# A hybrid decoder layer on one core: experts taken four at a time instead of one by one

## Chip, cores and metric

One core of a Trainium2 chip. The metric is the device time of one execution in microseconds; the median of the runs counts.

## What is computed

One decoder layer over 256 tokens of width 1024, all in float32: a token mixer (sparse attention beside a recurrent branch), and then a mixture of 32 experts with two chosen per token. The change lies in the second part and in the step between the two:

```python
h = h + gt1 * (merged @ w_out[l])
xn2 = _rmsnorm(h, moe_norm_g[l]) * (1.0 + sc2) + sh2
moe = _hier_moe(xn2.reshape(B * S, D), ...)
h = h + gt2 * moe.reshape(B, S, D)

def _hier_moe(xt, wg_router, we_router, e_bias, w_gate, w_up, w_down):
    ...
    def body(acc, ew):
        wg, wu, wd, cw = ew
        hdn = jax.nn.silu(xt @ wg) * (xt @ wu)
        return acc + cw[:, None] * (hdn @ wd).astype(f32), None
    acc, _ = lax.scan(body, jnp.zeros((T, D), f32), (w_gate, w_up, w_down, combine.T))
```

Gate and up weights are 1024 x 512 for each expert, down weights 512 x 1024: 6 MiB an expert, 192 MiB in all.

## The kernel before, in words

*Memory and loads.* One big tile, the arena, holds nearly everything, and a planner in the kernel's own text gives out columns of it while the program is built (`Arena.alloc`). Weights come in a fixed list of loads of 1 MiB (2048 float32 columns in 128 partitions), issued on the SP queue by `pump` (L271 to L287, the DMA at L283) as soon as a place is free; `done` gives a load's place back and pumps again. An instruction on SP that waits for its place holds up all that stand behind it. Two more tiles, both called `more`, join the arena when the mixer's buffers end. The list's last part is the experts: gate in two halves, up in two halves, and then, one expert late, down in two halves; for the last expert the down halves are columns instead of rows (2 KB pieces instead of 8 KB).

*Between mixer and experts.* The output projection runs in 16 steps of twelve products of 128x256 (L520 to L522), its weights split beforehand into a high and a low part by ACT, DVE and POOL, four pairs ahead. The logits of the router (L1465) and the sum of squares (L1467) run beside it. A step `reorder` stands after the fifth of these steps: 16 small products (L1485) and a few DVE operations bring shift and scale of the second norm into another order of channels. Then come the turns of the residual to token rows (L1473), and the routing, a long chain of small DVE operations (L1556 to L1606).

*The experts.* Each expert has room for 32 tokens (`CAP`); an overflow loop after them is empty here. For every four experts `group` makes a one-hot matrix and gathers their tokens by products (`gather`, L1620, 16 products, shown as 32 records, since a float32 product is two records in the profile) into eight slices of 128 columns, 32 for each expert. Then, expert by expert: `gate_up` runs 16 products of 128x512 in TensorE's four column groups (L1645), two for gate and two for up, each half of the contraction; ACT copies them, `hidden` turns them by products (L1652) and applies the SwiGLU on DVE and ACT; `scatter_weights` makes the matrix that brings rows back to tokens (L1634 on POOL, L1636); `down` runs 8 products (L1667), multiplies with the gate of the residual (L1672), and `finish` adds the expert's rows to the tokens in PSUM (four products of 128x512, L1699). The last expert's down products go by columns (`down_cols`, L1678, L1679), and `finish` adds the residual (L1701) and stores.

*What sets the order.* The program is recorded in the order of the text and a scheduling layer moves instructions within limits; SP's order is the list's. The first expert needs routing, the gather and the first four loads; a place comes free when the last product that reads it is over.

## Time and profile before

| | |
|---|---|
| runs | 805.62, 805.63, 882.06 us; median 805.63 |
| profiled execution | 806.51 us |
| its span, first to last instruction | 804.7 us |
| mean granted clock of TensorE | 0.959 of 2.4 GHz |
| busy | PE 694.5, DVE 382.7, ACT 201.4, POOL 216.4 us |
| HBM | 261.45 MB moved, 325 GB/s over the span |

The profile is of one execution. Sums are made against its 806.51 us and its span. The rows below show times in us from the span's start; a granted clock of 1.00 is 2.4 GHz and 0.50 is 1.2 GHz; a DMA share of 1 is all 16 DMA engines at work. Busy time of PE comes from records whose ends are modelled, so four products side by side in column groups show as overlapping records.

### The profile page before, as it was taken

How to read it: one execution, taken by the hardware profiler on the slowest of the kernel's cores; microseconds unless marked ns; L12 is line 12 of the kernel's file. 1: busy time of each engine (PE TensorE's matmuls, PEld its weight loads, DVE VectorE, ACT ScalarE, POOL GpSimd, SP SyncE). 2: the span in 40 equal slices, each digit the busy share in tenths (PEclk: the TensorE clock that was granted, in tenths of full speed). 3: DMA queues.
4: the chain of work that ended last, by engine and by line, in shares of the span. 5: the costliest groups of instructions: out<-in, count | busy, mean ns of one | idle time of the engine just before them, and what ended most of it. 6: DMA issues, size and time to landing. Idle time of an engine off the chain costs nothing.

```text
span 804.7 us, 12679 instructions
## 1 busy us (share of the span) xinstructions
PE 694.5 (86%) x5013; PEld 418.0 (52%) x5013; DVE 382.7 (48%) x866; ACT 201.4 (25%) x438; POOL 216.4 (27%) x251
## 2 busy tenths in 40 slices
PE   5898767899899999989998969888788779788777
PEld 1786547567789898954444324343243234243222
DVE  2577899999848666334223542221221221221214
ACT  2465523334536433231111101111011001011000
POOL 1348847612744226401111001101101101101100
PEclk9899968999999999989999989999999999999999
DMA  9995414456788566649999999999999999999994
GB/s 334 386 302 182 157 53 131 144 211 213 260 283 286 198 235 248 231 165 407 421 421 420 422 421 421 419 421 421 421 421 420 423 420 421 421 420 422 420 418 155
DMA packets 62636, 261.45 MB, mean 325 GB/s; under 512 B 7760, under 2 KB 23120, under 8 KB 36208
## 3 DMA queue, kind: packets, MB, share of 16 engines
q1 hardware_dynamic: 62576, 260.63, 82.4%
q8 instruction: 40, 0.66, 0.3%
q14 instruction: 20, 0.16, 0.1%
HBM read 259.57 MB, written 1.05 MB: 324 GB/s over the span
## 4 chain that ended last, share of the span: by engine, by line
PE 44%; DMA 32%; DVE 16%; POOL 4%; issue 2%; ACT 1%; DVEq 0%; SPq 0%; POOLq 0%
DMA arena<-in_expert_w_gate_dram 10%; DMA arena<-in_expert_w_up_dram 10%; PE ps_e L1645 7%; PE acc L1699 6%; DMA arena<-in_expert_w_down_dram 5%; PE ps_a L554 3%; PE ps_e L1620 3%; PE ps_e L1667 3%; PE ps_g L520 3%; DMA more<-in_expert_w_up_dram 3%; DMA more<-in_expert_w_gate_dram 2%; PE ps_g L522 2%; PE ps_g L521 2%; DVE split L510 2%; PE ps_e L1652 2%
## 5 line engine op out<-in xcount | busy, mean ns | idle before, releaser
L1634 POOL TENSOR_SCALAR arena<-arena 128x128 f32<-128x128 f32 x64 | 52.2, 822 | 373.8 <-PE ps_e L1636 213.6
L1645 PE MATMUL ps_e<-arena 128*32 128x512 f32 x832 | 134.5, 601 | 16.7 <-DMA arena<-in_expert_w_up_dram 16.7
L1699 PE MATMUL acc<-arena 128*128 128x512 f32 x256 | 119.9, 611 | 31.6 <-DVE arena L1672 31.6
L1699 PEld LDWEIGHTS acc<-arena 128*128 128x128 f32 x256 | 46.7, 193 | 98.2 <-DVE arena L1672 50.0
L1655 DVE TENSOR_SCALAR arena<-arena 128x128 f32<-128x128 f32 x32 | 7.2, 226 | 171.9 <-ACT arena L1654 171.6
L1646 ACT COPY arena<-ps_e 128x512 f32<-128x512 f32 x32 | 18.8, 586 | 279.2 <-PE ps_e L1645 279.2
L1645 PEld LDWEIGHTS ps_e<-arena 128*32 128x32 f32 x832 | 31.9, 110 | 93.8 <-issue 59.2
L510 DVE TENSOR_TENSOR split<-arena,split 128x512 fp32r<-128x512 f32 x84 | 67.2, 807 | 23.3 <-ACT split L509 12.6
L507 POOL TENSOR_SCALAR split<-arena 128x512 fp32r<-128x512 f32 x50 | 39.6, 796 | 103.1 <-PE ps_g L521 29.6
L1667 PE MATMUL ps_e<-arena 128*32 128x512 f32 x400 | 62.2, 601 | 0.5 <-DMA arena<-in_expert_w_down_dram 0.5
L1672 DVE TENSOR_TENSOR arena<-ps_e,arena 128x512 f32<-128x512 f32 x62 | 40.3, 683 | 45.6 <-PE ps_e L1667 45.5
L1645 PE MATMUL ps_e<-more,arena 128*32 128x512 f32 x192 | 57.5, 606 | 2.7 <-DMA more<-in_expert_w_up_dram 2.7
L554 PE MATMUL ps_a<-split 128*128 128x256 f32 x360 | 51.6, 303 | 2.9 <-ACT split L466 1.9
L554 PEld LDWEIGHTS ps_a<-split 128*128 128x128 f32 x360 | 47.6, 204 | 10.3 <-issue 4.8
L1652 PEld LDWEIGHTS ps_e<-arena 128*128 128x128 f32 x256 | 31.1, 191 | 27.0 <-ACT arena L1646 25.7
L509 ACT CAST split<-arena 128x512 fp32r<-128x512 f32 x60 | 36.5, 616 | 33.4 <-PE ps_g L521 17.0
L522 PE MATMUL ps_a<-split 128*128 128x256 f32 (+1 forms) x112 | 37.4, 334 | 8.1 <-DVE split L510 4.2
L1620 PEld LDWEIGHTS ps_e<-arena,more 128*128 128x128 f32 x256 | 33.4, 206 | 16.7 <-ACT arena L1637 6.9
L1620 PE MATMUL ps_e<-arena,more 128*128 128x128 f32 x256 | 35.7, 294 | 7.0 <-DVE arena L1692 5.6
L510 POOL TENSOR_TENSOR split<-arena,split 128x512 fp32r<-128x512 f32 x26 | 36.1, 1392 | 15.1 <-ACT split L509 11.2
L520 PE MATMUL ps_g<-split 128*128 128x256 f32 x128 | 39.0, 305 | 0.0
L521 PE MATMUL ps_a<-split 128*128 128x256 f32 (+1 forms) x112 | 36.4, 325 | 2.6 <-POOL split L510 1.0
(358 smaller groups left out, 1265.6 us busy)
## 6 DMA issues: line engine op xcount, KB each, us to landing
arena<-in_expert_w_up_dram SPq DMA_DIRECT2D x52, 1024.0 KB, 19.8
arena<-in_expert_w_gate_dram SPq DMA_DIRECT2D x52, 1024.0 KB, 19.8
arena<-in_expert_w_down_dram SPq DMA_DIRECT2D x52, 1024.0 KB, 19.8
arena<-in_w_in_dram SPq DMA_DIRECT2D x18, 1024.0 KB, 8.8
arena<-in_ada_w_dram SPq DMA_DIRECT2D x16, 1024.0 KB, 6.0
more<-in_expert_w_up_dram SPq DMA_DIRECT2D x12, 1024.0 KB, 19.8
more<-in_expert_w_down_dram SPq DMA_DIRECT2D x12, 1024.0 KB, 19.8
more<-in_expert_w_gate_dram SPq DMA_DIRECT2D x12, 1024.0 KB, 19.9
```

The source lines that it names most:

```text
L510: (nc.gpsimd if p[1] == "P" else nc.vector).tensor_sub(l, w, h.bitcast(F32))
L520: nc.tensor.matmul(ps, l[0], r[0], start=start, stop=False)
L521: nc.tensor.matmul(ps, l[0], r[1], start=False, stop=False)
L522: nc.tensor.matmul(ps, l[1], r[0], start=False, stop=stop)
L554: nc.tensor.matmul(p, a[:, kk, :], b[:, 4 * hf + kk, :], start=(i == 0 and kk == KORD[0]), stop=(i == 2 and kk == KORD[-1]))
L1620: nc.tensor.matmul(ps[:, n * kk:n * kk + n], h2[:, a, 2 * k2 + kk, :], oh(a), start=(a == 0), stop=(a == 1))
L1634: nc.gpsimd.tensor_scalar(o4[:, a], io1[:, None, :].to_broadcast([128, 4, CAP]), rk_(a), cb(a), op0=OP.is_equal, op1=OP.mult)
L1645: nc.tensor.matmul(ps[32 * g:32 * g + 32, :], xg[:, kk, :], w[:, k, :], start=(k == 0), stop=(k == 3))
L1652: nc.tensor.matmul(ps[:, 64 * f:64 * f + 64], gu[:, 128 * f:128 * f + 128], SEL, start=True, stop=True)
L1667: nc.tensor.matmul(ps[c][32 * g:32 * g + 32, :], hT[:, 2 * i + j, :], wd[:, j, 512 * c:512 * c + 512], start=True, stop=True)
L1672: nc.vector.tensor_mul(Y4b[:, s], ps[c], gt2[0][:, s])
L1699: nc.tensor.matmul(o, stb[e % 2][:, a, :], Y4b[:, s:s + n], start=(e == 0), stop=(e == NE - 1))
```

## The change

The list of loads goes by four experts: gate first halves of four, gate second halves, up first and second halves, down first and second halves. The last four have all their down weights in column halves. The four experts of a group now stand side by side in TensorE's column groups: `rows_in` accumulates gate in one PSUM tile of 128 rows (four experts x 32 places) and up in another, `hidden` works on 128 rows at once with tanh instead of exp and reciprocal, `turn_hidden` transposes, `rows_down` accumulates down products of the four, and `finish` brings all four back to tokens at once. The matrix for that is made once per four by one POOL product. The gather of the first four is cut in halves, each ahead of the products that need it. Several buffers of the expert stage are taken only when the first up weights are given back (`late`). The last columns run in two pairs of experts (`pairs_down`). The regrouping of shift and scale (`reorder`) is no longer in the projection; its DVE part stands ahead, its products (now 8) among the turns, its last two DVE operations in the routing.

```diff
-    for e in range(NE + 1):
...
+    for q in range(NE // 4):
+        for n, name, r in (("eg", "expert_w_gate", 4), ("eu", "expert_w_up", 4), ("ed", "expert_w_down", 2)):
             for i in range(2):
+                for e in range(4 * q, 4 * q + 4):
+                    w = I[name][0, e].rearrange("(p k) n -> p k n", p=128)
+                    if n == "ed" and q == NE // 4 - 1:
+                        add_load((n, e, i), (4, 512), [(None, w[:, :, 512 * i:512 * i + 512])])
+                    else:
+                        add_load((n, e, i), (r, 2048 // r), [(None, w[:, r * i:r * i + r, :])])
...
-        if j and m == 1:
-            after_last(lambda: None, False)
-            after_last(reorder)
...
     for m in range(8):
         turn(m)
+    psr = PS("a")
+    for k in range(8):
+        nc.tensor.matmul(psr[:, 16 * k:16 * k + 16], pick[:, k].rearrange("p m q -> p (m q)"), ss, start=True, stop=True)
+    A.free(h, sh2, s2c, ss, pick)
...
-    o4b = OHb = ME(2, 4, CAP)
-    sgb = ME(2, 4, CAP)
-    hTb = ME(4, CAP)
-    SEL = ME(64)
-    stb = [ME(2, 128), ME(2, 128)]
-    GUb = ME(512)
-    Y4b = ME(1024)
+    eqb, OHb, o4b = ME(2, 4, CAP), ME(2, 4, CAP), ME(2, 4, CAP)
...
+    t = ME(16, 8)
+    nc.vector.tensor_mul(t, psr[:, 0:128].rearrange("p (n m) -> p n m", m=8), blk[:, None, :].to_broadcast([128, 16, 8]))
+    nc.vector.tensor_reduce(both.rearrange("p k o -> p (k o)"), t, axis=AX.X, op=OP.add)
...
+    def rows_in(ps, xg, ws, i):
+        for k in range(4):
+            for g, w in enumerate(ws):
+                nc.tensor.matmul(ps[32 * g:32 * g + 32, :], xg[:, 4 * i + k, 32 * g:32 * g + 32], w[:, k, :],
+                                 start=(i == 0 and k == 0), stop=(i == 1 and k == 3))
+
+    def hidden(psg, psu, r):
+        nc.scalar.activation(thb[0:r], psg[0:r, :], AF.Tanh, scale=0.5)
+        nc.vector.scalar_tensor_tensor(thb[0:r], thb[0:r], 1.0, psg[0:r, :], op0=OP.add, op1=OP.mult)
+        nc.vector.scalar_tensor_tensor(hidb[0:r].rearrange("p (j q) -> p q j", j=4), thb[0:r].rearrange("p (q j) -> p q j", j=4),
+                                       0.5, psu[0:r, :].rearrange("p (q j) -> p q j", j=4), op0=OP.mult, op1=OP.mult)
...
+    def rows_down(pss, ws, i):
         for c in range(2):
+            for j in range(2):
+                for g, w in enumerate(ws):
+                    nc.tensor.matmul(pss[c][32 * g:32 * g + 32, :], hTb[:, 2 * i + j, 32 * g:32 * g + 32],
+                                     w[:, j, 512 * c:512 * c + 512], start=(i == 0 and j == 0), stop=(i == 1 and j == 1))
...
+    def pairs_down(ps, s, ws):
+        for jj in range(2):
+            for b, w in enumerate(ws):
+                for i in range(2):
+                    g = 2 * b + i
+                    nc.tensor.matmul(ps[32 * g:32 * g + 32, :], hTb[:, 2 * i + jj, s + 32 * b:s + 32 * b + 32],
+                                     w[:, 2 * i + jj, :], start=(jj == 0), stop=(jj == 1))
...
+    late = {("eu", 0, 1): late_hidden, ("eu", 1, 1): lambda: (gt2.append(ME(1024)), XGb.append(ME(8, 128))),
+            ("eu", 2, 1): late_rows, ("eu", 11, 1): late_tables}
...
+    for q in range(NQ):
+        es = range(4 * q, 4 * q + 4)
+        psg, psu = PS(), PS()
+        for n, ps in (("eg", psg), ("eu", psu)):
+            for i in range(2):
+                if q == 0 and n == "eg":
+                    fetch(0, range(2 * i, 2 * i + 2))
+                rows_in(ps, XGb[q % 2], [need((n, e, i)) for e in es], i)
+                for e in es:
+                    done((n, e, i), late.get((n, e, i)))
+        hidden(psg, psu, 128)
...
+        if q:
+            for c in (0, 512):
+                finish(stb[(q - 1) % 2], c, start=(q == 1))
...
+        turn_hidden(128)
+        pss = [PS(), PS()]
+        for i in range(2):
+            rows_down(pss, [need(("ed", e, i)) for e in es], i)
+            for e in es:
+                done(("ed", e, i))
+        for c in range(2):
+            times_gate(512 * c, pss[c])
...
+    cols_down(ps, [need(("ed", e, 0)) for e in es])
+    times_gate(0, ps)
+    finish(stb[(NQ - 1) % 2], 0, stop=True)
...
     for i in range(2):
+        ps = PS()
+        ws = [need(("ed", e, 1)) for e in es[2 * i:2 * i + 2]]
+        after_last(lambda: pairs_down(ps, 64 * i, ws))
+        times_gate(512, ps)
+        after_last(lambda: finish(st4[i], 512, stop=(i == 1)))
```

Where instructions now stand is shown at three places. The first is TensorE's row in the output projection and at its end. Before, the 16 small products of `reorder` (128x8) stand between two steps of the projection:

```order
L521 MATMUL ps_a<-split 128x256
L522 MATMUL ps_a<-split 128x256
L1485 MATMUL ps_g<-arena 128x8 x16
L520 MATMUL ps_a<-split 128x256
L521 MATMUL ps_a<-split 128x256
```

Now, at the projection's end (L1471 is a turn, L1463 a logit, L1465 the sum of squares, L1514 the regrouping, in the changed kernel's lines):

```order
L1463 MATMUL ps_r<-arena 128x36 x2
L1471 MATMUL ps_g<-arena 128x128
L1514 MATMUL ps_a<-arena 128x16 x3
L1471 MATMUL ps_g<-arena 128x128
L1465 MATMUL ps_r<-arena 128x1 x3
L1471 MATMUL ps_g<-arena 128x128
L1514 MATMUL ps_a<-arena 128x16 x2
```

Three of the eight products stand ahead of the last sum of squares, the others behind it.

The second place is the hand-over to the experts. TensorE before, from the last routing product on (L1620 gather, L1645 gate and up, L417 the broadcast of a gate, L1652 the hidden layer):

```order
L1592 MATMUL ps_g<-arena 128x32
L1620 MATMUL ps_e<-arena,more 128x128 x16
L1645 MATMUL ps_e<-arena 32x512 x16
L417 MATMUL ps_e<-arena 128x512 x2
L1652 MATMUL ps_e<-arena 128x64 x4
```

Now (L1604 gather, L1619 `rows_in`):

```order
L1573 MATMUL ps_g<-arena 128x32
L1604 MATMUL ps_e<-arena,more 128x128 x8
L1619 MATMUL ps_e<-arena 32x512 x16
L1604 MATMUL ps_e<-arena,more 128x128 x8
L1619 MATMUL ps_e<-arena 32x512 x33
```

Half of the gather now stands ahead of the first 16 products. SP's queue at the same place, before; the row of `arena` loads of down weights behind the `more` rows is the first that waits for an expert's products:

```order
L283 DMA more_3006<-in_expert_w_up_dram 128x2048
L283 DMA arena<-in_expert_w_down_dram 128x2048 x2
L283 DMA arena<-in_expert_w_gate_dram 128x2048 x2
L283 DMA more<-in_expert_w_up_dram 128x2048 x2
L283 DMA more<-in_expert_w_down_dram 128x2048
L283 DMA arena<-in_expert_w_down_dram 128x2048
```

Now:

```order
L281 DMA more_3006<-in_expert_w_up_dram 128x2048
L281 DMA arena<-in_expert_w_up_dram 128x2048 x2
L281 DMA arena<-in_expert_w_down_dram 128x2048 x2
L281 DMA more<-in_expert_w_down_dram 128x2048
L281 DMA arena<-in_expert_w_down_dram 128x2048
L281 DMA more<-in_expert_w_down_dram 128x2048 x2
L281 DMA arena<-in_expert_w_down_dram 128x2048 x2
L281 DMA arena<-in_expert_w_gate_dram 128x2048 x8
```

One more load, into a place of the arena that the turns set free, stands among the three into `more`; the two `arena` loads after those are the first to wait for an expert's products.

The third place is TensorE's end. Before (L1667 down of expert 30, L1678 down of expert 31 by columns, L1699 the return to tokens):

```order
L1667 MATMUL ps_e<-arena 32x512 x8
L1652 MATMUL ps_e<-arena 128x64 x4
L1636 MATMUL ps_e<-arena 128x128 x2
L1699 MATMUL acc_3410<-arena 128x512
L1699 MATMUL acc_3412<-arena 128x512
L1678 MATMUL ps_e<-arena 32x512 x4
L1699 MATMUL acc_3411<-arena 128x512
L1699 MATMUL acc_3413<-arena 128x512
L1678 MATMUL ps_e<-arena 32x512 x4
```

Now (L1632 the transposes of the hidden layer, L1768 the matrices of the two pairs, L1647 the first columns of all four experts, L1656 the pairs, L1696 the return):

```order
L1632 MATMUL ps_e<-arena 128x128 x4
L1768 MATMUL ps_e<-arena 128x128 x4
L1647 MATMUL ps_e<-arena 32x512 x16
L1656 MATMUL ps_e<-arena 32x512
L1696 MATMUL acc_3402<-arena 128x512
L1696 MATMUL acc_3404<-arena 128x512
L1656 MATMUL ps_e<-arena 32x512 x7
L1696 MATMUL acc_3403<-arena 128x512
L1696 MATMUL acc_3405<-arena 128x512
L1656 MATMUL ps_e<-arena 32x512 x8
L1696 MATMUL acc_3403<-arena 128x512
L1696 MATMUL acc_3405<-arena 128x512
```

Behind the last load there now stand eight products of a pair and two of the return.

## Rows read from the trace of the kernel before

**Rows 1.** The page: the chain by engine, and the group of the return

```profile
PE 44%; DMA 32%; DVE 16%; POOL 4%; issue 2%; ACT 1%; DVEq 0%; SPq 0%; POOLq 0%
...
L1699 PE MATMUL acc<-arena 128*128 128x512 f32 x256 | 119.9, 611 | 31.6 <-DVE arena L1672 31.6
```

**Rows 2.** Stretches: us, busy by engine (instructions), PE clock, DMA share, GB/s

```profile
351.00:356.00 5.00, 5.00 (x26) 5.00 (x25) 0.94 (x3) 0.81 (x2) 0.00 (x0) 0.50 0.03 13
356.00:361.00 5.00, 5.00 (x41) 2.01 (x41) 0.52 (x2) 1.28 (x3) 1.60 (x2) 1.00 0.00 0
370.00:787.00 417.00, 359.86 (x2190) 147.71 (x2188) 111.83 (x253) 46.49 (x117) 48.84 (x60) 0.99 1.01 420
```

**Rows 3.** SP's queue in order of time: start, us, what

```profile
342.67 0.42 SPq L283 DMA_DIRECT2D more<-in_expert_w_down_dram  x1
360.44 0.33 SPq L283 DMA_DIRECT2D arena<-in_expert_w_down_dram  x1
```

**Rows 4.** The chain in order of time: start, us, engine, tile, line

```profile
344.53 0.17 DVE arena L1556
...
350.29 6.52 PE ps_e L1620 x32
356.81 3.57 PE ps_e L1645 x32
...
468.27 5.55 PE acc L1699 x8
...
482.73 3.70 PE acc L1699 x8
```

**Rows 5.** Stretches at the end of the loads

```profile
787.00:792.00 5.00, 4.31 (x23) 1.90 (x22) 2.90 (x6) 0.68 (x3) 0.00 (x0) 1.00 0.58 222
791.00:792.00 1.00, 0.81 (x2) 0.00 (x0) 0.86 (x3) 0.00 (x0) 0.00 (x0) 1.00 0.22 84
792.00:794.00 2.00, 1.74 (x10) 0.67 (x11) 0.78 (x2) 0.00 (x0) 0.00 (x0) 1.00 0.01 5
```

**Rows 6.** The chain in the output projection, around the regrouping

```profile
318.66 3.60 PE ps_g L1485 x32
322.26 0.41 PE ps_a L520
322.68 0.21 PE ps_a L521
...
325.02 0.54 PE ps_r L1465 x4
...
325.76 0.12 PE ps_a L521
```

**Rows 7.** The stretch right behind the regrouping

```profile
322.00:325.00 3.00, 3.00 (x16) 3.00 (x15) 0.64 (x3) 0.00 (x0) 0.10 (x1) 0.50 1.01 423
```

**Rows 8.** TensorE in order of time, gate and up products at the lower clock

```profile
649.53 1.08 PE L1645 MATMUL ps_e<-arena 128*32 128x512 f32 x3
...
650.37 1.09 PE L1645 MATMUL ps_e<-arena 128*32 128x512 f32 x3
```

**Rows 9.** The page, DMA issues: KB each, us from issue to landing

```profile
arena<-in_expert_w_up_dram SPq DMA_DIRECT2D x52, 1024.0 KB, 19.8
```

**Rows 10.** The page, bandwidth in 40 equal slices of the span

```profile
GB/s 334 386 302 182 157 53 131 144 211 213 260 283 286 198 235 248 231 165 407 421 421 420 422 421 421 419 421 421 421 421 420 423 420 421 421 420 422 420 418 155
```

**Rows 11.** The end in order of time: last expert's columns, and the last add

```profile
792.26 1.06 PE L1678 MATMUL ps_e<-arena 128*32 128x512 f32 x8 [0.44 <-issue]
793.25 1.98 PE L1699 MATMUL acc<-arena 128*128 128x512 f32 x4
...
793.38 0.69 DVE L1679 TENSOR_TENSOR arena<-ps_e,arena 128x512 f32<-128x512 f32 x1 [1.22 <-PE ps_e L1678]
...
800.53 0.64 DVE arena L1701
```

**Rows 12.** Stretches around a wait of TensorE for DVE

```profile
465.00:468.00 3.00, 0.00 (x0) 0.00 (x0) 2.83 (x6) 0.00 (x0) 0.00 (x0) 0.53 1.03 429
468.00:471.00 3.00, 2.73 (x4) 1.19 (x5) 1.01 (x3) 0.00 (x0) 0.00 (x0) 0.50 1.02 423
471.00:474.00 3.00, 3.00 (x10) 1.15 (x12) 0.00 (x0) 0.00 (x0) 0.00 (x0) 0.83 1.00 410
```

More of the change, by code (lines that the diff above doesn't have):

```diff
@@ L1660, in down @@
-    def down(hT, wds, then=lambda i: None):
-        ps = [PS(), PS()]
-        for i, wd in enumerate(wds):
-            for c in range(2):
-                for j in range(2):
-                    g = 2 * (c ^ i) + j
-                    nc.tensor.matmul(ps[c][32 * g:32 * g + 32, :], hT[:, 2 * i + j, :], wd[:, j, 512 * c:512 * c + 512],
-                                     start=True, stop=True)
-            then(i)
-        for c in range(2):
-            s = slice(512 * c, 512 * c + 512)
-            nc.vector.tensor_mul(Y4b[:, s], ps[c], gt2[0][:, s])
@@ L1691, in group @@
         for a in range(2):
[L1692 to L1703 removed]
+            nc.vector.tensor_scalar(OHb[:, a], eqb[:, a], rs2[:, a:a + 1], None, op0=OP.mult)
@@ new lines, in fetch, with scatter, finish @@
+    def fetch(q, k2s=range(4)):
+        gather(XGb[q % 2], lambda a: OHb[:, a], 128, k2s)
+    def scatter(q):
+        nc.gpsimd.tensor_mul(o4b, eqb, comb[:, :, 4 * q:4 * q + 4][:, :, :, None].to_broadcast([128, 2, 4, CAP]))
+        ps = PS()
+        for a in range(2):
+            nc.tensor.transpose(ps[:, 128 * a:128 * a + 128], o4b[:, a].rearrange("p g s -> p (g s)"), ident)
+        nc.scalar.copy(stb[q % 2], ps[:, 0:256].rearrange("p (a t) -> p a t", a=2))
+    def finish(st, c, start=False, stop=False):
+        for a in range(2):
+            o = acc[2 * a + c // 512]
+            nc.tensor.matmul(o, st[:, a, :], Yb[:, c:c + 512], start=start, stop=stop)
+            if stop:
+                s = slice(c, c + 512)
+                nc.vector.tensor_add(y[:, a, s].rearrange("p (c k) -> p c k", k=8), o.rearrange("p (c k) -> p c k", k=8),
+                                     h2[:, a, :, c // 8:c // 8 + 64].rearrange("p k c -> p c k"))
+                nc.sync.dma_start(out=out[0, 128 * a:128 * a + 128, s], in_=y[:, a, s])
@@ L1723, in layer_kernel @@
             mod_bcast(gt2[0], row2, 2, 1.0)
             A.free(row2)
-        if e == NE - 1:
-            hT2 = ME(4, CAP)
-            y = ME(2, D)
+        if q == NQ - 1:
             break
-        if e:
-            down(hTb, [need(("ed", e - 1, i)) for i in range(2)], lambda i: done(("ed", e - 1, i)))
-        hidden(hTb)
-        scatter_weights(stb[i], o4b, lambda a: rk[:, a, e:e + 1], lambda a: comb[:, a, e:e + 1])
-        if e:
-            for c in (0, 512):
-                finish(e - 1, c, 512)
@@ L1736, in layer_kernel @@
-        if e % 4 == 2 and e < NE - 4:
-            group(e // 4 + 1)
-        if e == 8:
-            overflow_tables(nc, ovm, PS(), sel, rk, comb, ones, io)
-    last[0] = None
-    e = NE - 1
-    after_last(lambda: down(hTb, [need(("ed", e - 1, i)) for i in range(2)], lambda i: done(("ed", e - 1, i))))
-    after_last(lambda: hidden(hT2))
-    after_last(lambda: scatter_weights(stb[e % 2], o4b, lambda a: rk[:, a, e:e + 1], lambda a: comb[:, a, e:e + 1]))
-    after_last(lambda: finish(e - 1, 0, 512))
```

174 lines of the change are left out of this document (80 added, 94 removed).

## The prediction

> **What bounds the kernel now.** The chain that ended last is read first, and it misleads: it gives TensorE 44% and the transfers 32% [rows 1]. So the second view is the stretches. From 370 to 787 us the sixteen DMA engines stand at 1.01 of their time and move 420 GB/s, while PE is busy 359.86 of 417 us [rows 2]. Every piece of the chain in that stretch lies beside a full DMA, and work that leaves PE there moves nothing but PE's idle time. What can move the end is where the stream of expert weights starts, how much is left to load then, and what follows its last byte.
>
> The start is at a wall. After 351 us DMA share falls to 0.03 and then 0.00 while PE is busy all the time [rows 2]. The issues of the SP queue tell why: the last load before the experts leaves at 342.67, the next at 360.44 [rows 3]. Memory is full, and the first buffer comes free when the first expert's gate and up products end (356.81 + 3.57 us, [rows 4]). Of the 192 loads of 1 MiB (1.0486 MB) 21 are issued before that, 171 after. The last byte lands near 791.9: DMA still moves 84 GB/s from 791 to 792 and 5 after it [rows 5]. So 171 loads took 431.5 us, 2.52 us each (2.49 at 421 GB/s), and the program ends 12.8 us later, at the span's 804.7.
>
> **The change, part by part.**
>
> *Output projection and routing.* The regrouping of shift and scale leaves the projection, where it stood in PE's row for 3.60 us [rows 6]. It also cost what follows it: the granted clock is 0.50 from 322 to 325 us [rows 7], the 1.2 GHz level, after 16 matmuls of eight columns; the next twelve products take 0.21 us each and the logits 0.54, where after the return a product takes 0.12 [rows 6]. At the upper level these 2.76 + 0.54 us would be about 12 x 0.12 + 0.37 = 1.8, so 1.5 us more. Are the splits of the weights early enough for PE to run on? They work up to four pairs ahead, and the chain goes here from product to product without naming another engine; so I take the whole 5.1 us, and 3.6 as the other bound. Against it: the eight replacement products now stand among the turns, three of them ahead of the sum of squares for which routing waits. 32 records took 3.60 us, so six take about 0.7, on the path. On DVE a product and a reduction come into the chain of the inverse root, about 0.2 us each, as that chain's first step takes 0.17 [rows 4]. Together -5.1 + 0.7 + 0.4 = -4.0 us (bounds -2.5, and -5.1 if both additions are hidden).
>
> *First products.* Before, PE gathers all eight slices (6.52 us, clock 0.50 from 351 to 356) and only then takes 3.57 us of products: 10.1 us to the first release [rows 2, 4]. Now half of the gather, 3.26 us, precedes 32 records. PE's clock came back 5.7 us after the gather began; with the same delay 2.4 us of these products run at 1.2 GHz, where four records side by side take 0.84 us [rows 8], so about 11 records; the other 21 take 21/32 x 3.57 = 2.3. Sum 8.0, so -2.1 us. All at 1.2 GHz it is 3.26 + 6.7 = 10.0 (0), all at 2.4 GHz 3.3 us less. The releases that follow come every 4 to 6 us and bring four loads, 10 us of transfer; when the up products are done 14 loads are out, lasting some 35 us, and the first `rows_down` is over about 12 us later. No hole there, I expect.
>
> *Late buffers.* The buffers taken before the first expert shrink from 2752 columns to 768, and one load of 2048 columns fits in between: 22 loads go out before the first release. That load waits on SP for the turns, which run beside the start of routing, and two others stand behind it. Three loads are 7.5 us; from routing's first step to the first release it is 15.9 us before [rows 4] and 2.1 less now, so this costs nothing. One load less is left: -2.5 us (0 if it doesn't fit in time). Three buffers are taken back later, which leaves 20 loads in memory, as before.
>
> *By fours.* The number of expert products stays. Returns to tokens fall from 256 records to 32 plus a few; these 119.9 us [rows 1], the 64 comparisons on POOL and the reciprocals fall to about a quarter. I count nothing for it: the cover is the full DMA, and if that were gone the rival below gives the price. What could cost is release by fours. A load takes 19.8 us from issue to landing [rows 9], eight times 2.49, so eight are in flight. With 20 buffers at most 12 may lie landed and unreleased, so a batch (four loads) may be held some 20 us after it has landed. The worst place is the change of matrix: up products 3.6, return 3.7, gather and transposes about 5, some 3 us of ACT and DVE for the hidden layer, then 3.6 us of down products: 19 us after the up batch has landed, or 9 after the down batch. At 1.2 GHz this doubles for its first part only. Cost 0.
>
> *Last loads.* Eight loads now arrive as rows of 2 KB pieces instead of two. No stretch shows such a load alone; bounds are nothing and the whole slowdown of the last stretch but the drain. The near row is the early weights in small pieces, slice 2 of the page's bandwidth, 386 GB/s [rows 10]: 2.72 against 2.49 us, times six loads, 1.4. I take 1.0.
>
> *Tail.* After the last byte: sixteen records in four groups (eight take 1.06; the next eight, at 3.57/32 each, 0.9) 1.95 us, the gate 0.69 + 0.1, two sums 1.98 + 0.1 with the first add beside the second sum, the last add 0.64, then 3.5 us for store and exit as before (800.53 + 0.64 to 804.7) [rows 11]: 9.0 us. The pair before may still be in the sums when the byte lands, 0.4 us, and part of it may run at the lower level, 0.4: 9.8. So 9.8 - 12.8 = -3.0 us (bounds -3.8, 0).
>
> Sum: -4.0 - 2.1 - 2.5 + 0 + 1.0 - 3.0 = **-10.6 us**. The profiled execution took 806.51 us, 0.9 above the median of the runs, 805.63; 806.51 - 10.6 = 795.9 us, on the median's footing 795.0.
>
> **A rule that speaks against it.** The trace shows the clock falling when PE waits: 0.53 from 465 to 468 us, 0.50 to 471, 0.83 to 474 [rows 12]. The change makes such waits the rule: per batch 3.6 us of products in 10 us of transfer. The Trainium skill, TensorE: Matmul & The Clock Gate, section "HAM oscillation — how this bites in real kernels", says that bursts of products shorter than the wait for their data start throttled again each time. By that rule every batch takes up to twice 3.6 us, which still fits in 10, so the sum loses only what start and tail owe to the clock. The trace agrees as far as it goes: the return to tokens after that wait took 5.55 us instead of 3.70 [rows 4].
>
> **Rivals.**
> - *The clock stays low at both ends* (14%). The projection gains 2.5, the start nothing, the tail 0.5, the load 2.5, the pieces cost 1.4: 806.5 - 4.1 = 802.4 us. For it: 0.50 through the whole gather. Against: PE isn't idle at the end, batch on batch.
> - *All ends at their best* (10%): -5.1 - 3.3 - 2.5 - 3.8, and the drain from 787 to 792 us (222 GB/s, [rows 5]) 2.4 us shorter: 789.4 us. For it: fewer engines in each other's way. Against: the drain is DMA engines ending unevenly, which nothing here touches.
> - *TensorE bounds after all* (3%): then some 90 of the 119.9 us count, 806.5 - 90 = 716 us. For it the 44% of the chain, against it DMA at 1.01 throughout.
> - *Slower: PE can't follow at 1.2 GHz* (5%). Each four experts need 24 x 2.49 = 59.8 us of transfer. At the lower level PE needs six times 6.7, return 6.9, gather 6.5, transposes 2.3, so 56 us, and the waits for ACT and DVE between up and down products (4 us) bring it to the transfer's 59.8. From there on every us counts eight times; with 4 us more per four experts, 806.5 - 10.6 + 32 = 828 us. For it: the clock falls whenever PE waits some us [rows 12], and PE will wait in every batch. Against it: PE, busy again from 468 us, had its clock back within about 5 us [rows 12].
>
> **How the numbers follow.** The forecast has 68%, its own range 792 to 801 us. The rivals have 14, 10, 3 and 5%. Range 789.5 to 803: it takes in the first rival and the forecast's bounds and touches the second; left out are the last two and the edges. Over 2% (about what a measurement of this kernel can tell from no change) below 805.63 is under 789.5: the second and third rival, 13%. Over 2% slower is the last, 5%. Within: 82%.
>
> **What would show it.** In the profile of the changed kernel: twelve projection products at 0.12 us in place of the 3.60 us step; first release near 354 us; 22 expert loads issued before it; DMA at 420 GB/s from there to about 784; mean clock well below 0.959, with PE busy about half of each stretch; 9 to 10 us from last byte to end. Wrong it is if DMA drops below 1.0 between 370 and 780 us (release too late), or if the first release stays at 360.

## The result, and the profile after

| | before | after |
|---|---|---|
| median (20 runs each) | 804.44 us (800.95 to 882.06) | 797.38 us (796.32 to 805.8) |
| ratio, 95% interval | | 0.9918 (0.9891 to 0.9944) |
| profiled execution, span | 806.51, 804.7 us | 796.87, 795.1 us |
| mean granted clock | 0.959 | 0.932 |

The change gains 7.1 us between the medians, 0.8%: no difference by 2%, though the interval leaves 1.00 out. The ratios, here and below, leave out executions in a slow state (882.06 us of the kernel before, 819.23 us of "regrouping undone", two of the first "late buffers undone"); without them the medians of the first two are 804.17 and 799.34 us, and the gain is 6.8. The two profiled executions lie 9.6 us apart; why that is more is the first thing that the experiments settle.

The page after: what the engines did, the chain's first line, and the two groups of gate and up products. The columns are those of before.

```profile
PE 662.2 (83%) x4541; PEld 366.0 (46%) x4541; DVE 316.2 (40%) x704; ACT 176.2 (22%) x368; POOL 173.4 (22%) x205
...
GB/s 334 385 308 193 159 54 112 134 246 213 265 246 301 173 229 249 309 270 424 420 420 421 421 422 421 422 421 420 422 420 422 421 421 422 421 420 422 422 390 156
...
PE 2%; DVE 0%; issue 0%; DVEq 0%
```

Where before had 44% of PE and 32% of transfers in the chain [rows 1], the chain after holds only the last 24 us: followed back, it breaks off at 771 us. That it is short says nothing on what bounded the rest. The GB/s slices do: 420 to 424 from slice 19 to 38, as before [rows 10]; slice 39 has 390 where it had 418.

Stretches after (us, busy time by engine, PE clock, DMA share, GB/s), the start first, then the stream:

```profile
322.00:325.00 3.00, 3.00 (x27) 3.00 (x27) 1.37 (x3) 1.41 (x3) 1.50 (x2) 1.00 1.03 434
345.00:349.00 4.00, 2.98 (x15) 3.01 (x16) 2.16 (x12) 0.00 (x0) 0.62 (x1) 0.57 1.01 426
349.00:352.00 3.00, 3.00 (x32) 1.08 (x34) 0.27 (x1) 0.81 (x2) 0.00 (x0) 1.00 0.83 347
352.00:356.00 4.00, 4.00 (x40) 2.32 (x36) 1.18 (x4) 0.81 (x2) 0.00 (x0) 1.00 0.48 133
370.00:777.00 407.00, 327.92 (x1689) 99.24 (x1688) 48.01 (x97) 21.83 (x51) 8.24 (x14) 0.93 1.01 420
```

The first row stands against [rows 7]: clock 1.00 where it was 0.50, and 27 records where there were 16. The second and third stand against the low clock during the gather in [rows 2], the last against its third row: the DMA engines are as full as before, while PE is busy 81% of the stretch and not 86%, at a clock that has fallen from 0.99 to 0.93.

TensorE after, in order of time: the first and the last product of the output projection, and the first expert products (start, us, line, shape, records):

```profile
306.74 0.28 PE L518 MATMUL ps_a<-split 128*128 128x256 f32 x1
...
335.82 0.28 PE L520 MATMUL ps_a<-split 128*128 128x256 f32 x1
...
346.02 3.35 PE L1604 MATMUL ps_e<-arena,more 128*128 128x128 f32 x16 [1.31 <-DVE arena L1586]
349.31 3.64 PE L1619 MATMUL ps_e<-arena 128*32 128x512 f32 x32
352.88 2.05 PE L1604 MATMUL ps_e<-arena,more 128*128 128x128 f32 x16
```

and the SP queue there:

```profile
342.57 0.90 SPq L281 DMA_DIRECT2D more<-in_expert_w_down_dram  x2
352.96 0.80 SPq L281 DMA_DIRECT2D arena<-in_expert_w_down_dram  x2
```

The gather starts at 346.02 (before 350.29, [rows 4]), and the first buffer comes free at 352.96 (before 360.44, [rows 3]). 22 expert loads stand ahead of it, 21 before.

The chain after from 771 us to the end (start, us, engine, tile, line, records):

```profile
771.50 5.49 PE ps_e L1647 x31
...
777.46 0.70 DVE arena L1665
...
778.21 1.99 PE acc L1696 x4
780.19 1.88 PE ps_e L1656 x14
...
782.10 0.70 DVE arena L1665
782.80 0.14 issue
782.93 1.96 PE acc L1696 x4
784.89 1.90 PE ps_e L1656 x16
...
787.65 1.11 PE acc L1696 x2
...
788.78 1.04 DVE arena L1699
789.82 0.38 DVEq L1787
790.20 0.54 DVE arena L1699
```

No transfer stands in it. First-column products (L1647), their gate (L1665), their return (L1696), the first pairs (L1656), gate, return, last pairs, gate, return, add (L1699): all in series. The last byte lands near 781.9 us. Its place is hidden here by the first output stores, so it is taken as the release plus the 428.9 us that the stream takes where the stores come later (the run with the returns in another order, below). The second profile of the changed kernel shows it just ahead of its stores, and also 428.9 us after its release (352.66):

```profile
781.40:781.60 0.20, 0.20 (x8) 0.00 (x0) 0.20 (x1) 0.00 (x0) 0.00 (x0) 1.00 0.19 72
781.60:781.80 0.20, 0.20 (x7) 0.11 (x3) 0.20 (x1) 0.00 (x0) 0.00 (x0) 1.00 0.03 10
```

The last pairs start at 784.89 in the first profile, 3.0 us after the last byte.

### The profile page after: what moved, and what is told of

Its sections match the earlier page's. It is cut to its first block, busy times and chain, and to the rows that moved or that the text cites. A ratio compares the mean times of both kernels' runs of the same rounds, so it can differ in the third digit from the quotient of the medians.

```text
span 795.1 us, 11326 instructions
## 1 busy us (share of the span) xinstructions
PE 662.2 (83%) x4541; PEld 366.0 (46%) x4541; DVE 316.2 (40%) x704; ACT 176.2 (22%) x368; POOL 173.4 (22%) x205
## 5 line engine op out<-in xcount | busy, mean ns | idle before, releaser
L1619 PE MATMUL ps_e<-arena,more 128*32 128x512 f32 x440 | 92.5, 690 | 21.6 <-DMA arena<-in_expert_w_gate_dram 11.6
L1619 PE MATMUL ps_e<-arena 128*32 128x512 f32 x448 | 84.5, 652 | 22.3 <-DMA arena<-in_expert_w_gate_dram 12.4
L1640 PE MATMUL ps_e<-arena 128*32 128x512 f32 x360 | 85.6, 599 | 15.4 <-DMA arena<-in_expert_w_down_dram 11.4
L1686 POOL TENSOR_TENSOR arena<-arena 128x256 f32<-128x256 f32 x8 | 4.9, 617 | 283.3 <-PE ps_e L1689 281.6
L1625 DVE SCALAR_TENSOR_TENSOR arena<-arena,ps_e 128x512 f32<-128x512 f32 x8 | 5.5, 688 | 142.6 <-ACT arena L1624 142.6
L1665 DVE TENSOR_TENSOR arena<-ps_e,more 128x512 f32<-128x512 f32 x17 | 11.7, 691 | 124.4 <-PE ps_e L1640 110.1
L1624 ACT ACTIVATE arena<-ps_e 128x512 f32<-128x512 f32 x8 | 4.8, 597 | 248.3 <-PE ps_e L1619 248.3
L1619 PEld LDWEIGHTS ps_e<-arena,more 128*32 128x32 f32 x440 | 19.6, 122 | 81.4 <-issue 37.1
L1619 PEld LDWEIGHTS ps_e<-arena 128*32 128x32 f32 x448 | 18.8, 118 | 75.4 <-issue 34.6
L552 PEld LDWEIGHTS ps_a<-split 128*128 128x128 f32 x360 | 47.4, 203 | 10.4 <-issue 4.9
L1640 PEld LDWEIGHTS ps_e<-arena 128*32 128x32 f32 x360 | 19.5, 109 | 70.4 <-DMA arena<-in_expert_w_down_dram 32.8
L1626 DVE SCALAR_TENSOR_TENSOR arena<-arena,ps_e 128x512 f32<-128x512 f32 x8 | 8.2, 1030 | 88.5 <-PE ps_e L1619 88.5
L508 POOL TENSOR_TENSOR split<-arena,split 128x512 fp32r<-128x512 f32 x26 | 36.2, 1395 | 14.1 <-ACT split L507 10.3
L518 PE MATMUL ps_g<-split 128*128 128x256 f32 x128 | 39.3, 307 | 0.0
L520 PE MATMUL ps_g<-split 128*128 128x256 f32 x128 | 37.1, 289 | 0.0
L1604 PEld LDWEIGHTS ps_e<-arena,more 128*128 128x128 f32 x256 | 31.1, 199 | 12.8 <-issue 8.6
```

Source lines behind the costliest of these rows:

```text
L508: (nc.gpsimd if p[1] == "P" else nc.vector).tensor_sub(l, w, h.bitcast(F32))
L518: nc.tensor.matmul(ps, l[0], r[0], start=start, stop=False)
L520: nc.tensor.matmul(ps, l[1], r[0], start=False, stop=stop)
L552: nc.tensor.matmul(p, a[:, kk, :], b[:, 4 * hf + kk, :], start=(i == 0 and kk == KORD[0]), stop=(i == 2 and kk == KORD[-1]))
L1604: nc.tensor.matmul(ps[:, n * kk:n * kk + n], h2[:, a, 2 * k2 + kk, :], oh(a), start=(a == 0), stop=(a == 1))
L1619: nc.tensor.matmul(ps[32 * g:32 * g + 32, :], xg[:, 4 * i + k, 32 * g:32 * g + 32], w[:, k, :], start=(i == 0 and k == 0), stop=(i == 1 an ...
```

## Experiments

Twelve runs, in three groups of four; each group ran beside runs of the kernel before. The table is of the profiled executions, and most of what follows is read from it. "First" and "last" are the starts of the first and the last product of the output projection; "release" is the first issue on the SP queue that waits for an expert buffer, as in [rows 3]; "rest" is the span less the release; "loads" is how many expert loads leave before it. The median and the ratio are of each kernel's runs against those of before in its own group; each group ran on a chip of its own.

| kernel | first | last | gather | release | loads | span | rest | median | ratio |
|---|---|---|---|---|---|---|---|---|---|
| before | 307.31 | 341.51 | 350.29 | 360.44 | 21 | 804.7 | 444.3 | 804.44 | |
| before, again | 304.52 | 337.19 | 345.98 | 354.82 | 21 | 798.9 | 444.1 | (one run, 800.78) | |
| after | 306.74 | 335.82 | 346.02 | 352.96 | 22 | 795.1 | 442.1 | 797.38 | 0.9918 |
| after, again | 306.33 | 333.92 | 344.12 | 352.66 | 22 | 795.8 | 443.1 | 798.52 | 0.9914 |
| after, third | 306.50 | 335.57 | 345.76 | 352.80 | 22 | 795.0 | 442.2 | 796.59 | 0.9876 |
| only by fours | 307.19 | 336.55 | 345.33 | 355.50 | 21 | 800.2 | 444.7 | 803.91 | 0.9997 |
| returns four times | 307.31 | 334.88 | 345.08 | 352.19 | 22 | 794.3 | 442.1 | 798.17 | 0.9919 |
| regrouping undone | 305.04 | 339.26 | 348.05 | 355.42 | 22 | 797.5 | 442.1 | 799.87 | 0.9926 |
| half gather undone | 308.44 | 336.01 | 347.15 | 355.87 | 22 | 798.8 | 442.9 | 799.43 | 0.9917 |
| both undone | 306.53 | 337.43 | 346.22 | 356.50 | 22 | 798.3 | 441.8 | 798.14 | 0.9898 |
| late buffers undone | 306.81 | 334.38 | 344.58 | 351.61 | 21 | 796.4 | 444.8 | 798.67 | 0.9915 |
| tail, other order | 306.53 | 334.12 | 344.32 | 352.51 | 22 | 793.1 | 440.6 | 796.45 | 0.9892 |
| tail, filled | 306.02 | 333.60 | 343.80 | 351.89 | 22 | 795.1 | 443.2 | 797.24 | 0.9890 |

The 95% intervals of the ratios reach 0.0025 to 0.0037 to either side, 2 to 3 us. The row "late buffers undone" is the second of two runs of it.

**The two kernels once more.** No edit.

> The kernel before, unaltered, for a second profile. Theory P (the regrouping itself lowers the clock): the granted clock from 322 to 325 us is near 0.50 again and the first release falls near 360.4 us. Rival C (the low clock in the projection was that execution's, and comes and goes): the clock from 322 to 325 is near 1.00, the regrouping step takes about 1.9 us and not 3.6, the first release falls near 357 us, and the profiled time is near 802 and not 806.5 us.

> The changed kernel unaltered, for a second profile and as the measure for the others of this set. Theory S (start): the end is the first release of a buffer by the experts (352.96 us in the first profile) + 170 loads at 2.52 us + a tail of about 13 us, so 797 us again, ratio 0.99 to before, first release 352 to 355. Rival P (TensorE's own work by fours is what gained): the same time. If the first release is several us later in this profile, the time should follow it one for one.

> The changed kernel once more, unaltered, to stand beside the next three on one chip. Expected: first release of an expert buffer near 352.7 us, span some 442.5 us longer than that, median of the runs 797.5 to 799 us.

The kernel before, profiled again, released its first buffer at 354.82 and not 360.44 us, and ended 5.8 us sooner with the same rest. So the execution on which the prediction was built was a late one. Both theories had a part right. The regrouping takes as long at the full clock (32 records in 3.64 us, against 3.60 on the chain of before, [rows 6]), which was not what C said, and the clock falls behind it again, as P said. Of the 5.6 us at the release 2.8 were there at the first product of the projection, ahead of any place in which the regrouping stands; 1.5 came in the projection, which took 34.20 us from its first product to its last and here 32.67, with a second low stretch, 0.50 from 315 to 318 us in the first execution and 1.00 here; and 1.3 came between gather and release. The first and the last product of the projection, in the first execution and in the second:

```profile
307.31 0.28 PE L520 MATMUL ps_a<-split 128*128 128x256 f32 x1
...
341.51 0.28 PE L522 MATMUL ps_a<-split 128*128 128x256 f32 x1
```

```profile
304.52 0.28 PE L520 MATMUL ps_a<-split 128*128 128x256 f32 x1
...
337.19 0.28 PE L522 MATMUL ps_a<-split 128*128 128x256 f32 x1
```

TensorE and stretches of this second execution:

```profile
314.19 3.64 PE L1485 MATMUL ps_g<-arena 128*128 128x8 f32 x32
```

```profile
315.00:318.00 3.00, 3.00 (x28) 3.00 (x28) 0.14 (x1) 0.50 (x2) 1.95 (x2) 1.00 0.93 325
318.00:322.00 4.00, 4.00 (x23) 4.00 (x22) 1.68 (x5) 0.42 (x1) 1.33 (x2) 0.57 1.01 426
```

The changed kernel released at 352.66 and 352.80 in its two repeats.

**Only by fours.** The start and the late buffers are put back; experts by fours, side by side, the order of loads, the 2 KB pieces and the pairs at the end stay.

```diff
+        if j and m == 1:
+            after_last(lambda: None, False)
+            after_last(regroup)
...
+    thb, hidb, hTb, stb = ME(512), ME(512), ME(4, 128), [ME(2, 128), ME(2, 128)]
+    Yb = ME(1024)
...
-                if q == 0 and n == "eg":
-                    fetch(0, range(2 * i, 2 * i + 2))
+                if q == 0 and n == "eg" and i == 0:
+                    fetch(0)
```

> The experts stay by fours, but three other parts are undone: the regrouping of shift and scale is back in the projection, the first gather is whole, the late buffers are taken before the first expert (21 loads ahead of the first release instead of 22). Theory S: first release near 360 us, 171 loads of 2.52, tail 13: as before the change, ratio 1.00 (+-0.004), about 7 to 10 us above the changed kernel. Rival P: the saved returns and small operations remain, so most of the gain remains: ratio 0.992 or below.

0.9997 (0.9970 to 1.0025): no gain that shows, with the larger part of the change by far in place, most of the 119.9 us of returns [rows 1] among it. The changed kernel's median is 5.4 us lower on the same chip, so most of the gain is in the three small edits. The release at 355.50 is one early execution's: its 802.03 us lie 1.9 below the median. The regrouping here is eight products of sixteen columns (1.85 us), not the sixteen of eight of before, so part of the gain is left in: its projection takes 29.36 us against 32.67 and 34.20 before, its rest is 0.5 us longer. The medians, 0.9 us apart, don't show those 3 us or so; whether the by-fours part takes some of them back, this run doesn't settle.

**Returns four times.** For the first 28 experts the rows are summed into the result four times, so their part of the output counts fourfold.

```diff
-            for c in (0, 512):
-                finish(stb[(q - 1) % 2], c, start=(q == 1))
+            for r in range(4):
+                for c in (0, 512):
+                    finish(stb[(q - 1) % 2], c, start=(q == 1 and r == 0))
```

> The return to tokens of the first 28 experts is summed four times over (the output is wrong by that: their rows count four times), 7 x 3 x 3.44 = 72 us more of TensorE work inside the stream of loads. Theory S: DMA stays full, first release and last byte unchanged, time within 1.5 us of the changed kernel. Rival P: TensorE's work counts, up to 72 us more; half of it would be 36 us.

```profile
370.00:777.00 407.00, 369.59 (x1851) 123.64 (x1849) 47.68 (x97) 21.86 (x50) 8.21 (x14) 0.97 1.01 419
```

The returns alone are busy 107.35 us in the stretch, 27.77 in the changed kernel. PE as a whole is busy 41.7 us more and not 72, since the clock is 0.97 in place of 0.93 and the other products get shorter. The DMA share is the same, and so is the time (0.9919 against 0.9914 on the same chip). TensorE's work beside the stream was free here: this is why the work that the by-fours part saves is worth nothing, and it ends the rival "TensorE bounds after all".

**Parts of the start, undone.** First the regrouping, with its sixteen products of eight columns:

```diff
+            for o in range(2):
+                nc.tensor.matmul(psr[:, 16 * k + 8 * o:16 * k + 8 * o + 8], pick[:, k].rearrange("p m q -> p (m q)"), ss[:, o],
+                                 start=True, stop=True)
...
+        if j and m == 1:
+            after_last(lambda: None, False)
+            after_last(regroup)
```

> The changed kernel, but with the sixteen products of eight columns that regroup shift and scale back inside the output projection. Theory P (these products and the low clock behind them held up the start): the projection ends about 4 us later, the first release of an expert buffer falls near 356.7 us in place of 352.7, and the time is about 4 us above the changed kernel, 802 to 803 us. Rival C (the clock falls in the projection with or without them, because TensorE waits there for the split of a weight; only the products' own time counts): the granted clock from 322 to 325 us may stay at 1.00, the step takes 1.9 us at the upper level, the release falls near 354 us and the time is 1.5 to 2 us above, about 800 us.

Then the whole gather ahead of the first products (`fetch(0)`, as in the diff of "only by fours"):

> The changed kernel, but with the whole gather of the first four experts ahead of the first products. Theory: the second half of the gather, sixteen records, stands before the first release again. At 1.2 GHz that half is 3.3 us, at 2.4 GHz about 2: the first release falls between 354.7 and 356.0 us in place of 352.7, the last byte and the end move by as much, 800 to 801.5 us. Rival: the release is set by the transfers of the first gate weights or by the clock's return, and not by the gather; then release and time stay within 0.5 us.

And both, with the regrouping as eight products:

> The changed kernel with both parts of the start undone: eight products that regroup back inside the output projection, and the whole gather ahead of the first products; the late buffers stay late (22 loads). Theory A (the span is the first release plus a constant, and a load less before it is 2.5 us): the three undone together took 803.9 us, so this one takes 801.4, release near 355.5 us or a little later, release to end 442.5 us. Rival (one undone part costs nothing, two do: the clock's return covers one of them): 803 to 804 us, with the release near 358 us.

The clock is as P said: with the regrouping in the projection, this kernel's stretches read

```profile
318.00:322.00 4.00, 4.00 (x20) 4.00 (x21) 0.99 (x3) 0.00 (x0) 0.57 (x1) 0.50 1.01 424
322.00:325.00 3.00, 3.00 (x17) 3.00 (x17) 0.77 (x2) 0.61 (x2) 0.78 (x2) 0.58 1.01 426
```

and 1.00 in the second one in the changed kernel. In the profiles the release came 2.6, 3.1 and 3.7 us after the changed kernel's 352.8, each time with the rest unchanged. But the first product of the projection, which stands ahead of all that was undone, lay at 305.04, 308.44 and 306.53 us. Counted from it, the release comes after 50.4, 47.4 and 50.0 us, and after 44.8 to 46.3 (mean 45.8) in the seven executions with the changed kernel's start: 4.6, 1.7 and 4.2 us later. For the regrouping that is what P said, for the gather it is less than the 2 to 3.3 expected. The third is no sum of the first two, since its eight products lengthen the projection by 1.8 us (29.36 against 27.58, 30.90 against 29.08 with the second low stretch in both), where sixteen take 5.1 (32.67 against 27.58) or more. The medians moved less than the profiles: 0.9926 and 0.9917 against 0.9914 and 0.9918, 0.9898 against 0.9876. With intervals of 2 us and more these ratios can't price one part; the table can. Of the times expected, 802 to 803, 800 to 801.5 and 801.4, no median reached one.

**Late buffers undone.** Run twice, the second time for its profile.

```diff
+    thb, hidb, hTb, stb = ME(512), ME(512), ME(4, 128), [ME(2, 128), ME(2, 128)]
+    Yb = ME(1024)
...
-    thb = hidb = hTb = stb = Yb = None
...
```

> The changed kernel, but with the five buffers of the hidden layer and of the results taken before the first expert, so that 21 loads leave before the first release and not 22. Theory: first release unchanged near 352.7 us, one load more behind it, so everything from there to the last byte is one load of 2.5 us longer: 800.5 to 801 us. Rival: the number of loads before the release doesn't count, since the stream is never short of buffers afterwards and the end is set by TensorE's row from 771 us on, which starts when the down weights of the last experts land; then under 1 us.

> The changed kernel with the five buffers taken before the first expert again, for a profile. Theory A: 21 loads before the first release, the release itself near 352.7 us, and release to end 445 us where the changed kernel has 442 to 443; the median 2 to 2.5 us above the changed kernel's. Rival: release to end within 1 us of 442.5, the median within 1 us of the changed kernel's.

The queue in the second of them:

```profile
334.70 1.28 SPq L281 DMA_DIRECT2D more<-in_expert_w_down_dram  x3
351.61 1.28 SPq L281 DMA_DIRECT2D arena<-in_expert_w_down_dram  x3
```

21 loads before the release, and a rest of 444.8 us, as theory A said. The medians agree in sign: 0.9924 in the second group, and 2.1 us above the changed kernel in the third (0.9915 against 0.9876).

**The tail in another order.** The pairs of the first two experts go ahead of the return of the first columns, which needs nothing that is late.

```diff
-    finish(stb[(NQ - 1) % 2], 0, stop=True)
...
+        if i == 0:
+            after_last(lambda: finish(stb[(NQ - 1) % 2], 0, stop=True))
```

> Same as the changed kernel, but at the end the products of the first pair of experts stand ahead of the return of the first columns, so that PE doesn't wait for the gate of those columns. Theory S with a tail that is a row of work on TensorE (from the first-column products at 771.5 on PE works or waits for the gate, and the last pair starts 2.9 us after the last byte): about 2 to 2.5 us less than the changed kernel. Rival: the tail is set by the last byte's landing, then no change (within 0.5 us in the profile).

The chain of this kernel, from the last weights that the first-column products wait for:

```profile
756.68 14.76 DMA arena<-in_expert_w_down_dram
...
771.49 5.63 PE ps_e L1647 x25
...
777.55 1.72 PE ps_e L1656 x13
779.27 3.63 PE acc L1696 x8
782.90 1.90 PE ps_e L1656 x16
...
788.21 0.54 DVE arena L1699
```

The gate now runs beside the returns. Counted from the release, the last pairs start 1.5 us sooner than in the changed kernel (430.4 against 431.9), and the end comes 1.5 us sooner (440.6 against 442.1; 2.5 against its second profile). The transfers did not change, so from 771.5 us on the tail is TensorE's row and not the last byte; where that row starts is set by a transfer, as most of the first-column products wait here for their weights. The last byte can be seen, near 781.45: DMA moves 78 GB/s from 781 to 781.5 and 4 in the half microsecond after. The median of this kernel, 796.45 us in six runs, is the lowest here, but the changed kernel has 798.52 in the same group and 796.59 in the third, and the intervals overlap. Only the rest shows a gain: 440.6 in one execution, where the seven with 22 loads and the changed kernel's tail have 441.8 to 443.1.

**The tail filled.** On top of that order, products into an unused bank, to keep the clock up.

```diff
+    def fill(n):
+        ps = PS()
+        for k in range(n):
+            nc.tensor.matmul(ps, stb[(NQ - 1) % 2][:, 0, :], Yb[:, 0:512], start=True, stop=True)
+
+    fill(5)
...
+    fill(5)
```

> The changed kernel with the first two experts' pairs ahead of the return of the first columns, and ten products of 512 columns into an unused bank while TensorE waits for the transposes and the last down weights (the output doesn't read them). Theory (the tail is TensorE's own row from 771 us on, run partly at 1.2 GHz): the first-column products start with the clock at 1.00 and take 3.5 us and not 5.6, the last pair starts within 0.5 us of its last byte, and release to end falls from 440.6 to about 439 us; median near 795 us. Rival (the last byte alone sets the end): release to end stays at 440.5 us or more.

```profile
776.08 3.57 PE ps_e L1647 x32
779.65 1.72 PE ps_e L1656 x16
781.36 3.63 PE acc L1696 x8
784.99 1.90 PE ps_e L1656 x16
```

A miss that shows both sides: at the full clock the first-column products take 3.57 us and not 5.49, but ten filling products are twenty records, 9.1 us, more than the wait that they were to fill. The real ones start at 776.08, 4.6 us later than the 771.49 of the run before. The rest is 443.2.

## Why the prediction was right, and where not

The forecast, 795.9 us in a range of 789.5 to 803, holds the 797.38, and the difference is within 2%. The sum behind it was not right to the same degree: it said -10.6 us, and the medians moved by 7.1 (6.8 without the execution named above). The steps, each against the table:

- *What bounds the kernel* (the start of the stream, the number of loads, what follows the last byte; not TensorE): right. In thirteen executions the span is the release plus 440.6 to 444.8 us, while the release itself runs from 351.6 to 360.4. "Returns four times" and "only by fours" show the same from the other side.
- *Projection and routing, -4.0*: right. The projection is to be counted from its own first product, which lies anywhere from 304.5 to 308.4 us in the thirteen executions. From there to its last product it takes 27.57 to 27.59 us in six executions without the small products and 29.07 and 29.08 in two, which have the second low stretch: that stretch costs 1.5. With the sixteen products of before it takes 32.67, and 34.20 with the second low stretch. Like against like that is -5.1 both times, what was taken for products and clock ("regrouping undone" has 34.22 without that stretch: its clock is low from 318 to 325 us). From there to the gather it is 8.78 or 8.79 us in each of the five executions with the regrouping in the projection, and 10.20 in the seven with it among the turns ("half gather undone" had 11.1, with the clock at 0.50 from 340 to 345 us): +1.4 where 1.1 was taken. Together -3.7.
- *First products, -2.1*: right. From the gather's start to the release it is 8.7 to 10.3 us with the whole gather (five executions, mean 9.6) and 6.9 to 8.5 with half of it (eight, mean 7.5): -2.1.
- *Late buffers, -2.5*: right. By fours the rest is 444.7 and 444.8 with 21 loads, and 442.3 on average over the seven executions with 22 and the changed kernel's tail: -2.4. That the waiting load hides behind routing holds too, as the gather starts no later with it: 37.77 us after the first product of the projection without it, 37.77 to 37.79 with it in the four executions that also lack the second low stretch.
- *By fours, 0*: right as to TensorE's work, as "returns four times" shows. That the other costs of release by fours are nothing is not shown as closely: the rest is 0.5 us longer, and 0.9997 holds some of the start's gain.
- *Last loads in 2 KB pieces, +1.0*: the rate fell as the near row said, the sum didn't. The stretch of those loads after:

```profile
756.00:760.00 4.00, 2.01 (x4) 0.18 (x2) 0.00 (x0) 0.00 (x0) 0.00 (x0) 0.80 1.01 404
760.00:764.00 4.00, 3.42 (x17) 0.69 (x20) 0.00 (x0) 0.00 (x0) 0.00 (x0) 0.50 1.04 386
764.00:768.00 4.00, 2.88 (x18) 0.52 (x11) 1.02 (x1) 0.00 (x0) 0.00 (x0) 0.84 1.05 387
```

  386 and 387 GB/s, the value of [rows 10]. But 170 loads from release to last byte took 428.9 us, 2.52 each as before (781.45 - 352.51, in the run with the tail's other order, whose loads are the same, and 781.6 - 352.66 in the changed kernel's second profile). The DMA engines end more together: before, the rate fell from 787 us on, 5 us ahead of the last byte [rows 5]; after, from 778, 4 us ahead. That the one pays for the other is worked out and not shown by a run of its own.
- *Tail, -3.0*: the step that failed. It took 9.8 us from the last byte to the end, with "the pair before may still be in the sums when the byte lands, 0.4" and 0.4 for a lower clock. Measured: 13.2, and 14.2 in the second profile, against 12.8 before. The last pairs start 3.0 us after their last byte (4.0 in the second), since TensorE has a row of its own ahead of them that the sum left out: first-column products (5.5 us, at a clock of 0.57 from 772 to 776), return, pairs, gate and return of the first two experts, from 771.5 to 784.9 without a gap but the gates. Then 5.9 us to the end of the last add, where 5.5 was taken, and 4.4 to the span's end in place of 3.5. The bound of that term, 0, was nearer than the term; the order of the tail is worth 1.5 us or more of it, as the run shows.

With these sizes: -3.7 - 2.1 - 2.4, and +0.5 for fours, pieces and tail together (rest 444.2 before, 444.75 by fours with 21 loads): -7.7 us. The medians' 7.1 lies beside it, and the interval of the ratio, 4.5 to 8.8 us, holds both. The second step that failed is not in the sum. It stood on an execution that released at 360.44, late even for its kernel: the median of 20 runs is 2.1 us below its 806.51. So the two errors partly cancelled in the time: 3.5 too much gain, from a start 2.1 too high. That 795.9 came within 1.5 us is in part luck.

Of the rivals, "the clock stays low at both ends" came nearest: the tail gained nothing, and the clock was part of that. It was wrong for the projection and the start. "TensorE can't follow" did not come: DMA is at 1.01 from 370 to 777 us, with the clock at 0.93.

One sign that the prediction named failed beside the tail: PE was to be busy about half of each stretch, and it was 81%. A batch is no short burst here. Its first products run as each load lands, and the rest when the last one has:

```profile
516.22 1.04 PE L1619 MATMUL ps_e<-arena,more 128*32 128x512 f32 x2 [0.34 <-DMA arena<-in_expert_w_up_dram]
518.71 1.04 PE L1619 MATMUL ps_e<-arena,more 128*32 128x512 f32 x2 [1.45 <-DMA arena<-in_expert_w_up_dram]
521.19 3.62 PE L1619 MATMUL ps_e<-arena,more 128*32 128x512 f32 x26 [1.44 <-DMA arena<-in_expert_w_up_dram]
```

The granted clock of the stream fell as the prediction expected, 0.99 to 0.93 with PE waiting in and between batches, and stood at 0.97 when "returns four times" gave it more to do. It did not fall at every batch: in slices of 2 us from 370 to 760 us it lies below 0.75 in ten places, of 2 to 8 us each, while some forty batches of 10 us pass; it is 0.50 from 500 to 504 us and 1.00 from 521 to 524, in the batch shown. The Trainium skill, TensorE: Matmul & The Clock Gate, "HAM oscillation — how this bites in real kernels", has products in bursts shorter than their wait for data start throttled each time. The trace agrees in part, and adds where it counts: nowhere in the 420 us under a full DMA, and 1.9 us (5.49 against 3.57) at the tail, where TensorE's row is the path.

What stays open: by the medians, undoing the parts of the start one by one or together costs 0 to 2 us, by the profiles, counted from the first projection product, 1.7 to 4.6. Only the profiled executions have rows, and each kernel's runs spread over 3 to 12 us. No run shows why the first product of the projection lies up to 4 us apart from one execution to the next.

## What to carry to other kernels

Where one full resource bounds a kernel, find the event at which its long stretch starts, and write the time as that event plus a constant; then each edit either moves the event, shortens the stretch or does nothing, and most of a large rewrite may do nothing. What follows the last byte must be laid beside the row of the engine that receives it: ask when that engine gets there, not only what it does then. Before summing against one profile, see from the spread of the runs, or from a second profile, whether it was an early or a late execution. And when two profiles are compared, count from an event just ahead of the edit: from the start of the span the 5.1 us of this projection look like 4.5 (339.3 against 334.8 us, the means of the table's last products), and two undone parts that cost 4.6 and 1.7 look like 2.6 and 3.1.

## What the runs showed of the hardware

- The granted clock fell to 0.50 to 0.58 at the end of sixteen products of eight columns, or just behind them, in all three executions that had them in the projection, with PE busy all the time. Behind eight products of sixteen columns in the same place it did not, in both executions (1.00 and 0.98 in the next stretch).
- A second low stretch, 0.50 from 315 to 318 us, was there in some executions of the same kernel and not in others (before, after, "after, third" and "both undone" had it, the others 0.95 or 1.00). It comes behind three short waits of TensorE for POOL, ACT and DVE (0.3, 0.5 and 0.65 us), but the same waits stand in all thirteen executions, so they don't decide it alone. It leaves 16 records in those 3 us where "only by fours" has 28, and makes the projection 1.5 us longer (29.08 against 27.58).
- The release follows the gather's start less than one to one. Gathers that began at 343.8 to 344.3 took 8.1 to 8.5 us to the release, those at 344.6 to 348.1 took 6.9 to 7.4 (with half of the gather ahead of the first products). In the early ones the first 32 records of products took 4.4 to 4.8 us, partly at 0.50, in the others 3.6 to 3.7.
- Loads in 2 KB pieces moved 386 to 388 GB/s from 760 to 772 us; in the same 12 us of the kernel before, in longer rows, it was 420 to 426.
